# An opening in 176-token pieces with half weight blocks, and an ending in which the last two output blocks run by token half

## The chip, the cores and the metric

The kernel runs on all 8 cores of one Trainium2 chip, as two dies of four cores (cores 0 to 3 and 4 to 7). Each core computes half of one batch row, 2 × 1024 tokens, and the cores exchange nothing. The metric is the device time of the slowest core in microseconds (us).

Executions of this program fall into two states. In the slow state one die or both show a lower granted TensorE clock (as the profile records it, 1.00 being full speed), where the undisturbed runs have 0.996 to 0.999.

## The reference

One layer of a decoder trunk, in float32, with 16384 tokens of 2048 channels. The kernel works in bf16 on TensorE. What matters here is the first thing that is done and the last:

```python
def rmsnorm(x, g):
    y = x * lax.rsqrt(jnp.mean(x * x, axis=-1, keepdims=True) + EPS)
    return y * g

def swiglu_ffn(h, w_in, w_out):            # w_in: (2048, 2*5632), w_out: (5632, 2048)
    gate, up = jnp.split(h @ w_in, 2, axis=-1)
    return (jax.nn.silu(gate) * up) @ w_out

def reference(x, ...):                     # one layer
    x = x + 0.5 * swiglu_ffn(rmsnorm(x, ffn1_norm), ffn1_w_in, ffn1_w_out)
    x = x + mixer_block(rmsnorm(x, mix_norm), ...)      # [cut]
    x = x + 0.5 * swiglu_ffn(rmsnorm(x, ffn2_norm), ffn2_w_in, ffn2_w_out)
    return rmsnorm(x, final_norm)
```

The kernel must begin with the product of the norm of x with `ffn1_w_in`, and can end only after the last column of the last product has gone into the sum of squares of the final norm.

## The kernel before

Tokens lie along the free dimension and channels on the 128 partitions, so a token's sum of squares is a sum over 16 rows of channels and then over the partitions. The 16 rows are added by VectorE (or row by row on the way), and the partitions by a float32 matmul with a matrix of ones ("the sum" below). The norm factor is applied after the product, in the eviction from PSUM, so the product can begin with the raw x, only cast to bf16.

The opening takes x in three pieces of 352 tokens. Each weight block of 256 columns (1 MB in bf16) is one DMA.

```python
def x0_raw(s):                      # cast piece s into H (bf16): 12 rows on VectorE, 4 on ScalarE
    ...
def x0_sum(s, us):                  # squares on ScalarE, then adds of 4, 4, 4, 2, 1 rows on VectorE
    ...
    later(us, lambda: (pending.discard((0, s)), stats_finish(0, lo, hi)))   # the sum, root, reciprocal

x0_load(0)
first = [W.get(w1, 0, NKD, 0)]                       # one block of 256 columns
x0_load(1)
first += [W.get(w1, 0, NKD, DFF), W.get(w1, 0, NKD, 256), W.get(w1, 0, NKD, DFF + 256)]
x0_load(2)
x0_raw(0); x0_sum(0, 2.0); x0_raw(1)
# [cut] tiles in the order (block, piece), gate and up halves of two hidden blocks:
order = [(0, 0), (0, 1), (1, 0), (1, 1), (2, 0), (2, 1), (3, 0), (3, 1)]
order += [(w, 2) for w in range(4)]                  # piece 2 of all four blocks at the end
```

The ending is the last product, `ffn2_w_out` on the second 1024 tokens, in 8 blocks of 256 output columns. Blocks 0 to 6 run whole. Block 7 runs in three pieces of tokens, and the output of a piece is finished while TensorE works on the next one:

```python
cuts = (0, T // 2, T // 2 + 320, T)                  # pieces of 512, 320 and 192 tokens
# done(j, qs, bank): eviction with residual, square on ScalarE, add into RS on VectorE
# finish(q): the sum by ones, root, reciprocal;  final(q, sets): multiply 16 rows by RS, store
for q, (lo, hi) in enumerate(pieces):                # the last block
    for m in range(2):
        bank = nbank(True)
        for (k0, nk), ws in zip(kbs, wss):
            part(bank, ws, m, lo, hi, k0, nk)
            if q > 0 and m == 0 and k0 == 16:
                finish(q - 1)
                final(q - 1, sets[0:2])
        done(2 * cb + m, [q], bank)
        if q > 0 and m == 0:
            final(q - 1, sets[2:])                   # stands ahead of the eviction of m == 1
finish(npc - 1)
final(npc - 1, sets)
```

The program emits one list of instructions for each engine, with semaphores between the lists. In the traces below VectorE works off its list in the order of emission: on core 5 of after, casts whose data is there stand behind an eviction that waits 2.92 us.

Of the kernel before, what the change touches and what calls it, by code (L numbers as in the profile page):

```python
# [12 lines left out]
D = 2048  # L13
# [12 lines left out]
CUT = sorted({0, W0} | {c for g in GA + GB for c in g})  # L26
# [134 lines left out]
class WStream:  # L161
    def __init__(self, P, ring):
        self.P = P
        self.ring = ring
        self.n = 0
        self.bufs = [Buf(f"ring{i}") for i in range(RING)]
        self.semk = [P.newsem(f"ring{i}") for i in range(RING)]

    def get(self, wt, k0, nk, c0, reads=()):
        s = self.n % RING  # L170
        self.n += 1
        src = wt[c0 // 256, :, k0:k0 + nk, :]
        dst = self.ring[s]
        self.P.op(POOL, lambda e, dst=dst, src=src, nk=nk: e.dma_start(out=dst[:, 0:nk, :], in_=src),  # L174
                  reads=reads, writes=[self.bufs[s]], semkey=self.semk[s], incval=16)
        return s

    def pair(self, wt, cb, nk):
        s = self.n % RING
        self.n += 1  # L180
        src = wt[cb:cb + 2].rearrange("c p k n -> p c k n")
        dst = self.ring[s][:, 0:2 * nk, :].rearrange("p (c k) n -> p c k n", c=2)
        self.P.op(POOL, lambda e, dst=dst, src=src: e.dma_start(out=dst, in_=src),
                  writes=[self.bufs[s]], semkey=self.semk[s], incval=16)
        return s
# [14 lines left out]
def emit_program(nc, st, dr):  # L200
# [17 lines left out]
    ring = [sb(f"ring{i}", [128, 16, 256], BF16) for i in range(RING)]  # L218
# [24 lines left out]
    N0 = W0 // 3  # L243
    X0 = view(0, 48 * N0 * 4, F32, N0)
    b_X0 = [[region(f"X0{k}_{s}", (s * NKD + k) * 4 * N0, 4 * N0) for s in range(3)] for k in range(NKD)]
# [55 lines left out]
    s_x0 = [P.newsem(f"x0{s}{q}") for s in range(3) for q in range(4)]  # L301
# [3 lines left out]
    b_DW = {n: [Buf(f"d{n}_{c}") for c in range(8)] for n in ("WBc", "WBo")}  # L305
# [92 lines left out]
    def wcol(s, kc, m):  # L398
        return ring[s][:, kc, m * 128:(m + 1) * 128]

    def proj_H(ws, m, g):
        lo, hi = g
        bank = nbank()
        mms(bank, [(wcol(ws, k, m), H[:, k, lo:hi]) for k in range(NKD)],
            [W.bufs[ws]] + [b for k in range(NKD) for b in r_H[k].at(lo, hi)], True, True, hi - lo)
        return bank
# [62 lines left out]
    def to_bf16(src, dst, c):  # L469
        P.op(POOL, lambda e: e.dma_start(out=dr[dst][c], in_=dr[src][c]), writes=[b_DW[dst][c]], semkey=s_w,  # L470
             incval=16)
# [27 lines left out]
    def ffn_in(w_in, S, groups, first=None, hook=None, un=False, mid=None, conv=False, cast=()):  # L499
        tmps = {}  # L500

        def gate(ws, m, s):
            g = groups[s]
            n = g[1] - g[0]
            bank = proj_H(ws, m, g)

            def fn():
                t = mul_rs(bank, S, g) if un else None
                tmps[m, s] = t2 = t if un else ntmp()
                act(bank, tmp(t2, n), [b_TMP[t2]], AF.Silu, n, t=t)  # L510

            evac((S, s), bank, fn)
            run_bg()

        def up(ws, b, m, s):
            lo, hi = g = groups[s]
            n = hi - lo
            bank = proj_H(ws, m, g)
            j = 2 * b + m

            def fn():
                t = tmps[m, s]
# [12 lines left out]

        cast = deque(cast)
        if hook is None:
            first = [W.get(w_in, 0, NKD, 0), W.get(w_in, 0, NKD, DFF)]
            order = [(w, s) for s in range(len(groups)) for w in range(2)]
        else:  # L540
            order = [(0, 0), (0, 1), (1, 0), (1, 1), (2, 0), (2, 1), (3, 0), (3, 1)]
            order += [(w, 2) for w in range(4)]
        for i, (w, s) in enumerate(order):
            if hook is not None:
                hook(i)
            for m in range(2):
                if w % 2 == 0:
                    gate(first[w], m, s)
                else:
                    up(first[w], w // 2, m, s)  # L550
        for b in range(len(first) // 2, NKF // 2):
# [24 lines left out]
    def ffn_out(w_out, S, groups, src, dst, un_cg=None, hd=None, ahead=None):  # L576
        for cb in range(NKD // 2):
# [6 lines left out]
            for k0 in range(0, NKF, 16):  # L584
# [5 lines left out]
                for m in range(2):  # L590
                    j = 2 * cb + m
                    for s, (lo, hi) in enumerate(groups):
# [3 lines left out]
                            [W.bufs[ws]] + [b for k in range(nk) for b in r_A[k0 + k].at(lo, hi)],  # L596
# [15 lines left out]
    def ffn_out_last(w_out, S, src):  # L612
# [4 lines left out]
        nblk = 3 * NKD // 2  # L617
        spare = (W.n + nblk) % RING
        tw = TMP[:, NTMP - 2:NTMP, :].rearrange("p c t -> p (c t)")
        rows = [(ap[:, HALO:W0], bufs) for ap, bufs in rows]  # L620
        rows.append((ring[spare][:].rearrange("p k c -> p (k c)").bitcast(F32)[:, 0:T], [W.bufs[spare]]))
        rows.append((tw, b_TMP[NTMP - 2:NTMP]))
        state["tmp"] = 0
        cuts = (0, T // 2, T // 2 + 320, T)
# [14 lines left out]
        def done(j, qs, bank):  # L639
# [13 lines left out]
            else:  # L653
                t = turn("tmp", NTMP - 2)
# [19 lines left out]
        for j, n in ((0, 4), (4, 4), (8, 4), (12, 2), (14, 1), (15, 1)):  # L674
# [4 lines left out]
            elif j < 14:  # L679
                ap = sg[:, :, HALO:W0]  # L680
            else:
                ap = rows[j][0].unsqueeze(1)
# [17 lines left out]
        def part(bank, ws, m, lo, hi, k0, nk):  # L700
            lo, hi = lo + HALO, hi + HALO
            mms(bank, [(wcol(ws, k, m), ACTB[:, k0 + k, lo:hi]) for k in range(nk)],
                [W.bufs[ws]] + [b for k in range(nk) for b in r_A[k0 + k].at(lo, hi)],
                k0 == 0, k0 + nk == NKF, hi - lo)

        for cb in range(NKD // 2):
            last = cb == NKD // 2 - 1
            if last:
                wss = [W.get(w_out, k0, nk, cb * 256) for k0, nk in kbs]
            load(2 * cb)  # L710
            load(2 * cb + 1)
            if not last:
                halves = [(0, T // 2, [0]), (T // 2, T, list(range(1, npc)))]
                bk = [[nbank(True) for h in halves] for m in range(2)]
                for k0, nk in kbs:
                    ws = W.get(w_out, k0, nk, cb * 256)
                    for m in range(2):
                        for s, (lo, hi, qs) in enumerate(halves):
                            part(bk[m][s], ws, m, lo, hi, k0, nk)
                            if k0 + nk == NKF:  # L720
                                done(2 * cb + m, qs, bk[m][s])
                continue
            for q, (lo, hi) in enumerate(pieces):
                for m in range(2):
                    bank = nbank(True)
                    for (k0, nk), ws in zip(kbs, wss):
                        part(bank, ws, m, lo, hi, k0, nk)
                        if q > 0 and m == 0 and k0 == 16:
                            finish(q - 1)
                            final(q - 1, sets[0:2])  # L730
                    done(2 * cb + m, [q], bank)
                    if q > 0 and m == 0:
                        final(q - 1, sets[2:])
# [48 lines left out]
    def mix_a(S, hd):  # L782
# [125 lines left out]
        def grp(gi, ws):  # L908
            for m in range(2):
                j = 2 * gi + m  # L910
                for lo, hi in GB:
                    bank = nbank()
                    mms(bank, [(wcol(ws, 2 * gi + k, m), PLD[:, k, lo - HALO:hi - HALO]) for k in range(2)],
                        [W.bufs[ws]] + b_P, True, True, hi - lo)
# [15 lines left out]
        def pool_out(ws, j, g, i, gate, b_gate, k0=0):  # L930
            lo, hi = g
            bank = nbank()
            mms(bank, [(wcol(ws, k0 + k, j % 2), MX[:, k, lo:hi]) for k in range(8)],
                [W.bufs[ws]] + [b for k in range(8) for b in r_MX[k].at(lo, hi)], True, True, hi - lo)
# [25 lines left out]
        for j in range(12, NKD):  # L960
            i = turn("st", NST)
            for s, g in enumerate(GB):
                c = 2 * (j - 12) + s
                pool_out(wp, j, g, i, SG[:, c, :], b_SG[c], 8 * (j // 2 - 6))
# [76 lines left out]
    def mix_b(S, hd=None, un_cg=None):  # L1041
# [12 lines left out]
        for cb in range(8):  # L1054
            ws = W.get(dr["WBc"], 0, 8, cb * 256, [b_DW["WBc"][cb]])
            for m in range(2):
# [3 lines left out]
                for lo, hi in GB:  # L1060
# [4 lines left out]
                        [W.bufs[ws]] + [b for k in range(8) for b in cn(k)[1]], True, True, n)  # L1065
# [9 lines left out]
        for cb in range(8):  # L1075
# [3 lines left out]
            for m in range(2):  # L1079
# [3 lines left out]
                for k0, k1 in cuts:  # L1083
                    for s, (lo, hi) in enumerate(GB):
                        n = hi - lo
                        mms(bks[s], [(wcol(ws, k, m), MG[:, k, lo:hi]) for k in range(k0, k1)],
                            [W.bufs[ws]] + [b for k in range(k0, k1) for b in r_M[k].at(lo, hi)],
# [12 lines left out]
    def x0_load(s):  # L1100
        for q in range(4):
            P.op(POOL, lambda e, q=q: e.dma_start(  # L1102
                out=X0[:, s * NKD + 4 * q:s * NKD + 4 * q + 4, :], in_=dr["x0"][s, :, 4 * q:4 * q + 4, :]),
                writes=[b_X0[k][s] for k in range(4 * q, 4 * q + 4)], semkey=s_x0[4 * s + q], incval=16)

    def quad(s, q):
        k0 = s * NKD + 4 * q
        return X0[:, k0:k0 + 4, :], [b_X0[k][s] for k in range(4 * q, 4 * q + 4)]

    def x0_raw(s):  # L1110
        lo, hi = GA[s]
        for q in range(4):
            for k in range(4 * q, 4 * q + 4):
                src, b = X0[:, s * NKD + k, :], [b_X0[k][s], b_CST]
                if k % 4 == 3:
                    P.op(ACT, lambda e, k=k, src=src: e.activation(out=H[:, k, lo:hi], in_=src, func=AF.Copy,
                                                                   scale=cst(C_N1 + k)),
                         reads=b, writes=r_H[k].at(lo, hi))
                else:
                    vec(N0 / 2, lambda e, k=k, src=src: e.tensor_scalar(  # L1120
                        out=H[:, k, lo:hi], in0=src, scalar1=cst(C_N1 + k), scalar2=None, op0=ALU.mult),
                        b, r_H[k].at(lo, hi))

    def x0_sum(s, us):
        lo, hi = GA[s]

        def tree(n, out, in1, reads, writes):
# [175 lines left out]
```

## Time and profile before

| | |
|---|---|
| time, 3 fast runs | 5003.28, 5004.66, 5004.85 us (median 5004.66); a fourth run was slow, 5183.32 |
| profiled execution, slowest core 2 | span 5005.4 us (device time of this execution 5007.22) |
| spans of the 8 cores | 4997.5 to 5005.4 us, granted clock 0.996 to 0.998 |
| TensorE (PE) busy | 4933.7 us, 99% |

The head of the profile's page and the first group of its busy table:

```profile
span 5005.4 us, 63154 instructions; the slowest of 8 cores (4997.5 to 5005.4 us)
PE 4933.7 (99%) x24878; PEld 2477.3 (49%) x25230; DVE 1987.2 (40%) x2548; ACT 722.8 (14%) x1161; POOL 217.3 (4%) x414
```

TensorE is busy for 99% of the span, so only its idle time can be won without taking work away. The waits of TensorE, summed over the whole run of core 2, are few. The columns are the waiting line and tile, what it waited for, the total in us, how often, and the longest.

```profile
PE bank L392 <- DMA ring<-ffn_w_in: 21.9, 1, 21.9
PE bank L667 <- DVE RS L657: 12.6, 2, 7.7
PE bank L438 <- DVE RS L1128: 3.3, 1, 3.3
PE bank L392 <- DVE H L1120: 2.9, 1, 2.9
```

All of these lie at the two ends. The timeline of TensorE at the opening of core 2 follows. Its columns are start, duration, engine, line, operation, output and inputs, form, count, and in brackets the idle time before it with what ended it.

```profile
21.94 4.85 PE L392 MATMUL bank<-H,ring 128*128 128x352 bf16 x16 [21.94 <-DMA ring<-ffn_w_in]
...
33.12 11.39 PE L392 MATMUL bank<-H,ring 128*128 128x352 bf16 x64 [2.91 <-DVE H L1120]
47.83 1.32 PE L438 MATMUL bank<-RS,ONES 128*128 128x352 f32 x2 [3.31 <-DVE RS L1128]
48.94 11.24 PE L392 MATMUL bank<-H,ring 128*128 128x352 bf16 x66
```

The first matmul starts at 21.94 us, when its weight block has landed. After two more waits, for the casts into H and for the sum of squares (RS), TensorE is dense from 48.94 us on.

The same view at the ending, core 2:

```profile
4963.82 10.41 PE L392 MATMUL bank<-BIG,ring 128*128 128x320 bf16 x88
4981.96 1.40 PE L667 MATMUL bank<-RS,ONES 128*128 128x320 f32 x2 [7.73 <-DVE RS L657]
4983.16 6.71 PE L392 MATMUL bank<-BIG,ring 128*128 128x192 bf16 x56
4994.76 0.98 PE L667 MATMUL bank<-RS,ONES 128*128 128x192 f32 x2 [4.89 <-DVE RS L657]
```

The sums wait 7.73 and 4.89 us for RS. The timeline of VectorE (DVE) in the first of these waits tells why:

```profile
4969.66 4.49 DVE L692 TENSOR_TENSOR H<-H,RS 128x2048 f32<-128x2048 f32 x2
...
4975.64 2.28 DVE L692 TENSOR_TENSOR XS<-XS,RS 128x2048 f32<-128x2048 f32 x1
...
4979.57 0.68 DVE L692 TENSOR_TENSOR TMP<-TMP,RS 128x512 f32<-128x512 f32 x1
4980.18 0.48 DVE L647 SCALAR_TENSOR_TENSOR TMP<-bank,TMP 128x320 f32<-128x320 f32 x1
4981.32 0.49 DVE L657 TENSOR_TENSOR RS<-RS,TMP 128x320 f32<-128x320 f32 x1 [0.67 <-ACT TMP L655]
```

The bank with the last row of the 320-token piece is complete at about 4974.2 us (4963.82 + 10.41). Its eviction, the write into TMP at 4980.18, stands behind output multiplies of the 512-token piece (L692), for which TensorE is not waiting. The sum can start only after the add at 4981.32.

### The profile page before, as it was taken

What the parts mean: (1) busy time and instruction counts of PE and PEld (TensorE: products, weight loads), DVE (VectorE), ACT (ScalarE), POOL (GpSimd) and SP (SyncE); (2) the same over time, 40 slices, a digit from 0 to 9 for tenths busy, and PEclk for the clock granted to TensorE, in tenths of its full rate; (3) what the DMA queues carried; (4) which work ended last, traced back from release to release, by engine and by line L of the source; (5) the groups of instructions that cost most, each with busy time, mean ns of one, the idle gap of its engine ahead of it and who ended that gap; (6) DMA issues with size and microseconds to landing.
All of it is one profiled execution on the core that took longest, in us unless ns stands there. A gap on an engine that the chain in (4) does not pass through costs nothing.

```text
span 5005.4 us, 63154 instructions; the slowest of 8 cores (4997.5 to 5005.4 us)
## 1 busy us (share of the span) xinstructions
PE 4933.7 (99%) x24878; PEld 2477.3 (49%) x25230; DVE 1987.2 (40%) x2548; ACT 722.8 (14%) x1161; POOL 217.3 (4%) x414
## 2 busy tenths in 40 slices
PE   7999999999999999999999999999999999999998
PEld 4666666665444444444444444444444444444444
DVE  5344421289980000322568994001141533333113
ACT  3111111112110000121112210000020120000111
POOL 0000000000000000000000000000000000000000
PEclk9999999999999999999999999999999999999999
DMA  7768856545574444566766675344565754555544
GB/s 156 131 127 149 149 103 130 126 74 114 110 143 91 80 72 82 126 158 168 239 144 140 141 151 101 68 82 71 117 147 131 237 128 86 120 109 113 132 75 114
DMA packets 147795, 617.24 MB, mean 123 GB/s; under 512 B 14384, under 2 KB 37040, under 8 KB 107184
## 3 DMA queue, kind: packets, MB, share of 16 engines
q0 software_dynamic: 57632, 394.55, 45.5%
q1 hardware_dynamic: 89872, 218.64, 12.3%
q8 instruction: 204, 3.34, 0.3%
q14 instruction: 87, 0.71, 0.1%
HBM read 877.37 MB, written 109.05 MB: 197 GB/s over the span
## 4 chain that ended last, share of the span: by engine, by line
PE 98%; issue 1%; DVE 1%; DMA 1%; ACT 0%; POOL 0%; DVEq 0%; ACTq 0%; POOLq 0%
PE bank L392 97%; DMA BIG<-x 1%; PE bank L438 0%; DVE RS L671 0%; DVE BIG L1128 0%; DVE RS L448 0%; DVE H L692 0%; POOL BIG L1102 0%; PE bank L667 0%; ACT L446 0%; ACT BIG L1134 0%; DVE ST L692 0%; ACT TMP L655 0%; ACT RS L669 0%; DVE TMP L476 0%
## 5 line engine op out<-in xcount | busy, mean ns | idle before, releaser
L392 PE MATMUL bank<-H,ring 128*128 128x512 bf16 (+1 forms) x16852 | 3344.6, 358 | 40.0 <-DMA ring<-ffn_w_in 21.9
L392 PEld LDWEIGHTS bank<-H,ring 128*128 128x128 bf16 x17088 | 1673.6, 98 | 1692.0 <-issue 32.8
L392 PE MATMUL bank<-BIG,ring 128*128 128x512 bf16 (+2 forms) x7910 | 1584.1, 360 | 6.1
L392 PEld LDWEIGHTS bank<-BIG,ring 128*128 128x128 bf16 x8024 | 786.8, 98 | 795.2 <-issue 19.6
L792 DVE SCALAR_TENSOR_TENSOR BIG<-BIG,CST 128x1024 f32<-128x1024 f32 x480 | 595.5, 1277 | 0.0
L529 DVE TENSOR_TENSOR BIG<-bank,TMP 128x512 bf16<-128x512 f32 x176 | 121.8, 692 | 990.0 <-PE bank L392 989.9
L476 DVE TENSOR_TENSOR TMP<-bank,RS 128x512 f32<-128x512 f32 (+1 forms) x468 | 288.4, 617 | 405.5 <-PE bank L392 403.9
L600 DVE SCALAR_TENSOR_TENSOR XS<-bank,XS 128x512 f32<-128x512 f32 (+1 forms) x112 | 69.0, 616 | 538.8 <-PE bank L392 538.8
L524 DVE TENSOR_TENSOR TMP<-bank,TMP 128x352 f32<-128x352 f32 (+1 forms) x220 | 130.0, 591 | 382.6 <-PE bank L392 379.5
L489 ACT ACTIVATE TMP<-TMP 128x352 f32<-128x352 f32 (+1 forms) x220 | 120.3, 549 | 1027.6 <-DVE TMP L476 1027.5
L489 ACT ACTIVATE TMP<-bank 128x512 f32<-128x512 f32 x176 | 105.1, 597 | 1089.6 <-PE bank L392 1089.6
L433 DVE TENSOR_TENSOR RS<-RS,TMP 128x512 f32<-128x512 f32 (+1 forms) x223 | 143.2, 657 | 226.9 <-ACT TMP L431 226.9
L174 POOL DMA_DIRECT2D ring<-ffn_w_in x176 | 93.5, 532 | 2304.1 <-PE bank L392 2280.3
L526 DVE TENSOR_TENSOR BIG<-TMP,RS 128x352 bf16<-128x352 f32 (+1 forms) x220 | 130.4, 593 | 24.1 <-DVE TMP L524 2.4
L431 ACT ACTIVATE TMP<-XS 128x512 f32<-128x512 f32 (+1 forms) x147 | 83.2, 576 | 220.2 <-DVE XS L600 203.5
L489 ACT ACTIVATE TMP<-TMP,CST 128x512 f32<-128x512 f32 (+1 forms) x88 | 60.2, 685 | 344.7 <-DVE TMP L476 344.7
L174 POOL DMA_DIRECT2D ring<-ffn_w_out x96 | 50.7, 528 | 1216.1 <-PE bank L392 1191.2
L573 ACT ACTIVATE H<-XS,CST 128x352 bf16<-128x352 f32 (+1 forms) x56 | 34.0, 607 | 348.0 <-DVE XS L600 278.1
L448 DVE RECIPROCAL RS<-RS 128x512 f32<-128x512 f32 (+1 forms) x20 | 59.9, 3030 | 30.5 <-ACT RS L446 30.3
L489 ACT ACTIVATE ST<-TMP,CST 128x512 bf16<-128x512 f32 x64 | 46.2, 722 | 170.4 <-DVE TMP L476 164.9
L174 POOL DMA_DIRECT2D ring<-w_in x56 | 29.6, 528 | 791.6 <-PE bank L392 791.6
L647 DVE SCALAR_TENSOR_TENSOR H<-bank,H 128x512 f32<-128x512 f32 x16 | 11.1, 692 | 120.3 <-PE bank L392 120.3
(90 smaller groups left out, 893.9 us busy)
## 6 DMA issues: line engine op xcount, KB each, us to landing
ring<-ffn_w_in POOLq DMA_DIRECT2D x176, 1024.0 KB, 9.9
ring<-ffn_w_out POOLq DMA_DIRECT2D x64, 1024.0 KB, 10.1
ring<-w_in POOLq DMA_DIRECT2D x56, 1024.0 KB, 10.5
XS<-X SPq DMA_DIRECT2D x60, 512.0 KB, 12.2
X<-XS SPq DMA_DIRECT2D x56, 512.0 KB, 6.0
XS<-x SPq DMA_DIRECT2D x48, 512.0 KB, 10.4
ring<-ffn_w_out POOLq DMA_DIRECT2D x32, 768.0 KB, 7.6
ring<-WBo POOLq DMA_DIRECT2D x16, 1024.0 KB, 8.2
```

Of the source, the lines that this page charges most:

```text
L174: self.P.op(POOL, lambda e, dst=dst, src=src, nk=nk: e.dma_start(out=dst[:, 0:nk, :], in_=src), reads=reads, writes=[self.bufs[s]], semkey ...
L392: ins = e.matmul(d, w, r, start=(start and i == 0), stop=(stop and i == last))
L431: P.op(ACT, lambda e: e.activation(out=tmp(t, hi - lo), in_=src, func=AF.Square), reads=sbufs, writes=[b_TMP[t]])
L433: vec(hi - lo, lambda e: e.tensor_tensor(out=rs, in0=rs, in1=tmp(t, hi - lo), op=ALU.add), b_rs + [b_TMP[t]], b_rs)
L448: vec((hi - lo) * 6, lambda e: e.reciprocal(out=rs, in_=rs), b_rs, b_rs)
L476: vec(hi - lo, lambda e: e.tensor_tensor(out=tmp(t, hi - lo), in0=banks[bank][:, 0:hi - lo], in1=rsg(S, lo, hi), op=ALU.mult), [b_bank[ban ...
L489: P.op(ACT, lambda e: e.activation(out=out, in_=src, func=func, **kw), reads=[sbuf, b_CST], writes=obufs)
L524: vec(n, lambda e: e.tensor_tensor(out=tmp(t, n), in0=banks[bank][:, 0:n], in1=tmp(t, n), op=ALU.mult), [b_bank[bank], b_TMP[t]], [b_TMP[t]])
L526: vec(n, lambda e: e.tensor_tensor(out=ACTB[:, j, lo:hi], in0=tmp(t, n), in1=rsg(S, lo, hi), op=ALU.mult), [b_TMP[t]] + r_RS[S].at(lo, hi) ...
L529: vec(n, lambda e: e.tensor_tensor(out=ACTB[:, j, lo:hi], in0=banks[bank][:, 0:n], in1=tmp(t, n), op=ALU.mult), [b_bank[bank], b_TMP[t]], ...
L600: vec(n, lambda e, x=x, bank=bank, n=n: e.scalar_tensor_tensor(out=x, in0=banks[bank][:, 0:n], scalar=0.5, in1=x, op0=ALU.mult, op1=ALU.ad ...
L792: vec(T, lambda e: e.scalar_tensor_tensor(out=C[:, c, :], in0=G[:, j, 2 + t:2 + t + T], scalar=cst(C_CVK + j * KCONV + t), in1=C[:, c, :], ...
```

## The change

The intent is to start the first product sooner, with smaller first loads, and to keep TensorE from waiting for VectorE at the end. The cuts below are marked; the rest of the diff adapts names, buffers and the layout of the weights (blocks of 128 columns).

```diff
--- before, the opening
+++ after
-    N0 = W0 // 3                       # x in three pieces of 352 tokens
+    N0 = W0 // 6                       # six pieces of 176
...
+    def half(self, s, m, wt, c0):      # half a weight block, 128 columns, 512 KB in bf16
+        self.load(s, self.ring[s][:, m], wt[c0 // 128 + m], [self.bufs[s][m]], (self.semk, self.semh)[m][s])
...
-    x0_load(0)
-    first = [W.get(w1, 0, NKD, 0)]
-    x0_load(1)
-    first += [W.get(w1, 0, NKD, DFF), W.get(w1, 0, NKD, 256), W.get(w1, 0, NKD, DFF + 256)]
-    x0_load(2)
+    for what in ("x0", (0, 0), "x1", (1, 0), (0, 1), "x2", (1, 1), "x3", (2, 0), (3, 0), "x4", (2, 1), (3, 1), "x5"):
...
...                                     # cut: before, adds of 4, 4, 4, 2, 1 rows for 352 tokens
+            n = 8                       # per piece of 176 tokens: adds of 8, 4, 2, 1 rows
+            while n:
+                ...
+                n //= 2
...
+        tile(0, 0, 0)                   # tile(piece, block, half): 16 matmuls of 176 tokens
+        tile(1, 0, 0)
+        both(0, 1, 0)                   # both(p, ...): pieces 2p and 2p+1
+        both(0, 0, 1)
+        x0_raw(2)
+        x0_stats(0)
+        tile(2, 0, 0)
+        tile(2, 1, 0)
+        tile(2, 0, 1)
+        both(0, 1, 1)
+        tile(2, 1, 1)
+        x0_raw(3)
+        x0_sum(1)
+        tile(3, 0, 0)
+        ...
--- before, the ending
+++ after
-        cuts = (0, T // 2, T // 2 + 320, T)
+        cuts = (0, T // 2, T // 2 + 256, T // 2 + 416, T)
...
+        block(6, whole[0:1], w_late)    # first 512 tokens of blocks 6 and 7
+        block(7, whole[0:1], w_late)
+        bk = [nbank(True) for m in range(2)]
+        for k0, nk in kbs:              # second 512 tokens of block 6
+            ws = w_late(6, k0, nk)
+            for m in range(2):
+                part(bk[m], ws, m, T // 2, T, k0, nk)
+            if k0 == 0:
+                finish(0)
+                final(0, sets[0:2])     # the large multiply hides behind these matmuls
+            elif k0 == 16:
+                final(0, sets[2:])
+        for m in range(2):
+            done(12 + m, whole[1][2], bk[m])
+        wss = [w_late(7, k0, nk) for k0, nk in kbs]
+        for q in range(1, npc):         # second 512 tokens of block 7: 256, 160, 96
+            ...
--- before, ffn_in of the second ffn
+++ after
-    ffn_in(dr["ffn2_w_in"], 1, GB, un=True, mid=lambda: final_stream(0, 25.0))
+    ffn_in(dr["ffn2_w_in"], 1, GB, un=True, mid=lambda: final_stream(0, 25.0),
+           cast=[("ffn2_w_out", "WBf", c) for c in range(4)])    # last weights cast to bf16 in DRAM early
```

The work on TensorE stays the same in columns; the opening has twice as many matmuls, each half as wide, and the weights of blocks 6 and 7 are read twice.

## The prediction

> **Bound:** TensorE, busy 4933.7 of 5005.4 us (busy table); between 93.7 and 4902 us it is busy 4787 of 4808 us (windows). Only the two ends can win.
>
> *Opening* (timeline): the first matmul starts at 21.94, as the 1 MB weight block lands behind 2.9 MB of x. Before 49 us PE then waits 2.9 us for the VectorE casts into H and 3.3 us for the sum of squares; some runs cold (first 16 matmuls of 352 took 4.85 us, the next 16 2.55). From 48.94 it is dense; the first two weight pairs end at about 93.7.
>
> *Ending*: PE waits 7.73 and 4.89 us for the RS sums (PE waits), because VectorE runs the output multiplies (2.28 us each at 512 tokens) ahead of the evictions; the clock is then 0.64-0.67 (windows). The last product matmul ends at 4989.9, the span at 5005.4.
>
> **Opening after.** Source data arrived at about 0.34 MB/us (17 MB by 56 us). First tile needs 1.44 MB x and 1.05 MB weights: estimate 13.4 us instead of 21.9. But then VectorE paces. My estimate for a 176-token cast is 0.24 us (352: 0.34), so 2.9 us a piece, and 7.8 us for the adds of two pieces (1408-wide add 1.62, 704 0.89, 352 0.53). Walk: casts of piece 1 end 19; sums 0 and 1 end 29; casts of piece 2 end 32; reciprocal 2.35 and evictions; casts of piece 3 end about 44, with 36 of 48 tiles left at 1.21 us each (estimate 75.8 ns a matmul, from 148.8 at 352). Two sums and a wait for evictions (2-3 us) follow: end about 91 (88.5 to 94). Most of the 8.5 us is lost waiting for VectorE. Gain 2.7 us (0 to 7).
>
> [...]
>
> **Ending after.** Blocks 6 and 7 take the first half first, so the whole multiply of 512 tokens (about 13 us VectorE) hides behind block 6's second half (19 us). From the end of block 5 at 4901.8: three times 19.0, one sum 0.8, pieces 9.6 + 6.1 + 3.7 [...] plus two sums. VectorE walk for the tail: PE waits about 1 us before sum 2 and about 4.5 before the last sum; reciprocal of 96 about 0.75 (192: 1.35, 320: 2.15), one multiply and one output DMA fewer: end about 4994.5. Gain 11 us (7 to 13). The last weights (0.75 MB, 7.5 us landing) load while outputs move at about 340 GB/s; it may stall PE up to 3 us.
>
> **Middle.** Twice the weight descriptors, and four casts of 2.9 MB in the weight queue: nothing, landing is 10 us against over 19 us of slack.
>
> **Predicted: 4991 us, 80%: 4983 to 4998.** Faster by over 2%: 0.01; within 2%: 0.97; slower by over 2%: 0.02.
>
> **Shows it:** first matmul near 13.5; in PE waits, H casts and RS sums of opening total over 8 us; opening tiles end near 91; PE waits at the RS sums of the ending under 7 us in total; time from last product matmul to span end 12-13 us; matmul of 176 near 76 ns warm.
>
> **Wrong if:** narrow matmuls are bound by weight loads; 384-byte output rows slow the last stores; VectorE order stalls the opening more than walked.

The sum: 5005.4 − 2.7 − 11 is 4991.7. The 75.8 ns for a matmul of 176 tokens is an estimate; a line through two widths in the traces of before gives the same (1960 matmuls of 352 in 292.53 us on core 2, 149.2 ns each; 832 of 512 in 179.74 us on core 0, 216.0 ns).

## The result, and the profile after

The fast runs beside those of before took 4992.14 and 4993.49 us, and a further fast one 4993.38. Executions in which one die ran at a lower clock are left out of the means. The ratio of the fast runs is 0.9978, with a 95% interval of 0.9955 to 1.0: same at the 2% threshold. Ratios here are the mean time of one kernel's fast runs over that of the other's fast runs of the same rounds, so not quite the ratio of the medians that are quoted.

The slowest core of the profiled execution is core 5 (cores 4986.4 to 4990.6 us, granted clock 0.997 to 0.999):

```profile
span 4990.6 us, 64591 instructions; the slowest of 8 cores (4986.4 to 4990.6 us)
PE 4949.1 (99%) x25704; PEld 2503.6 (50%) x25704; DVE 1993.5 (40%) x2600; ACT 726.1 (15%) x1178; POOL 294.0 (6%) x428
```

Busy time of TensorE *rose* by 15.4 us while the span fell by 14.8. More matmul records are in this trace (25704, as many as weight loads; before has 24878 for 25230 weight loads), and a busy TensorE is not always at one rate (on core 5, 16 matmuls of 176 took 157 ns each from 14.14 us on and 128 took 77 each from 85.00), so the busy sum cannot tell what was gained. For that I split every execution at two places that are at the same position in the work in all kernels: "M1", the start of the first pair of 512-token sums after the opening's product (about 372 us), and the start of the last eviction of output row 11, the end of block 5 (about 4897 us). The three lengths, as means over the 8 cores of the profiled execution:

| | start to M1 | M1 to end of block 5 | end of block 5 to the end | sum |
|---|---|---|---|---|
| before | 372.07 | 4525.78 | 103.48 | 5001.34 |
| after | 372.68 | 4523.50 | 92.74 | 4988.93 |
| difference | +0.6 | −2.3 | −10.7 | −12.4 |

So the ending brought nearly everything, and the opening nothing. The −2.3 us in the middle does not look like the change's work: in this one execution of before, cores 0 to 3 took 4526.5 to 4529.0 us for the middle and cores 4 to 7 only 4523.8 to 4524.2, which is 1.8 us on the mean of all eight. The windows view of core 2 shows a granted clock of 0.92 from 2100 to 2170 us, where core 5 shows 1.00, with TensorE busy for 69.6 and 70.0 of the 70 us; core 2 of the kernel after shows 1.00 there. In windows of 10 us, cores 0 to 3 all show 0.81 from 2110 to 2120, and cores 2 and 3 once more from 2150 to 2160.

The waits of TensorE after, core 5:

```profile
PE bank L1186 <- DMA ring<-ffn_w_in: 14.1, 1, 14.1
PE bank L1186 <- DVE H L1143: 8.4, 3, 3.4
PE bank L675 <- DVE RS L665: 5.9, 2, 4.0
PE bank L1186 <- DVE TMP L487: 2.8, 1, 2.8
...
PE bank L445 <- DVE RS L1163: 1.1, 1, 1.1
```

The wait for the first weights fell from 21.9 to 14.1 us, and that for RS at the ending (L667, now L675) from 12.6 to 5.9. The opening's wait for its sums (L438, now L445) fell from 3.3 to 1.1. But its waits for casts into H went up from 2.9 to 8.4 us, and a wait for evictions (TMP) of 2.8 us is new there.

*Opening.* The timeline of TensorE, core 5; line 1186 holds the opening's tiles:

```profile
14.14 2.51 PE L1186 MATMUL bank<-H,ring 128*128 128x176 bf16 x16 [14.14 <-DMA ring<-ffn_w_in]
20.08 8.10 PE L1186 MATMUL bank<-H,ring 128*128 128x176 bf16 x80 [3.43 <-DVE H L1143]
...
32.01 10.15 PE L1186 MATMUL bank<-H,ring 128*128 128x176 bf16 x96 [1.93 <-DVE H L1143]
45.19 8.73 PE L1186 MATMUL bank<-H,ring 128*128 128x176 bf16 x96 [3.03 <-DVE H L1143]
...
59.76 24.78 PE L1186 MATMUL bank<-H,ring 128*128 128x176 bf16 x320 [2.79 <-DVE TMP L487]
...
85.00 9.87 PE L1186 MATMUL bank<-H,ring 128*128 128x176 bf16 x128
94.71 2.55 PE L399 MATMUL bank<-H,ring 128*128 128x352 bf16 x16
```

The first matmul starts 7.8 us earlier than on core 2 of before, and the product is dense only from 59.76 us instead of 48.94. The opening's tiles end at 94.71 us, on the mean of the cores at 93.44. Before they ended at about 92.9 on the mean (M1 less 279.2 us, the distance between the two places in the kernels that ran here).

What VectorE does before the longest of these waits, the one that ends at 45.19:

```profile
41.12 0.53 DVE L531 TENSOR_TENSOR TMP<-bank,TMP 128x352 f32<-128x352 f32 x1 [2.92 <-PE bank L1186]
41.75 0.53 DVE L533 TENSOR_TENSOR BIG<-TMP,RS 128x352 bf16<-128x352 f32 x1
42.19 2.74 DVE L1143 TENSOR_SCALAR H<-BIG,CST 128x176 bf16<-128x176 f32 x12
```

The casts of piece 3 (the 12 `TENSOR_SCALAR` at 42.19) stand behind the eviction at 41.12, and that has waited 2.92 us for a bank that TensorE was still filling. When TensorE has filled it, it has nothing left but tiles of piece 3, and now it waits for VectorE to evict and to cast. The two engines take turns. How long a turn lasts differs, and the clock has a part in it: on core 5 the granted clock read 0.50 from 32 to 36 us, and the 96 matmuls from 32.01 on took 10.15 us. On cores 0 and 2, at 1.00, they took 7.44 us; there VectorE idled 1.97 and 0.69 us in the same evictions, and both waits are put down to ScalarE (L500, a table load of 1.28 us and an activation of 0.50) and not to TensorE. So ScalarE is a link of the chain as well. On five of the eight cores, 1, 3, 4, 5 and 7, it is TensorE that the second of these evictions waits for (1.86 to 2.92 us). The order of VectorE's list shows here too: ScalarE's share of the casts of piece 3 ran at 38.70 us on this core without a wait for data, but VectorE's share only at 42.19, with 2.92 us of idle time on the way.

*Ending.* TensorE of core 5 and below it the output multiply of the 512-token piece on VectorE:

```profile
4943.48 24.90 PE L399 MATMUL bank<-BIG,ring 128*128 128x512 bf16 x188
...
4968.69 5.08 PE L399 MATMUL bank<-BIG,ring 128*128 128x160 bf16 x88
4975.68 0.51 PE L675 MATMUL bank<-RS,ONES 128*128 128x160 f32 x2 [1.91 <-DVE RS L665]
4976.03 3.08 PE L399 MATMUL bank<-BIG,ring 128*128 128x96 bf16 x44
4983.13 0.71 PE L675 MATMUL bank<-RS,ONES 128*128 128x96 f32 x2 [4.02 <-DVE RS L665]
```

```profile
4949.32 4.49 DVE L700 TENSOR_TENSOR H<-H,RS 128x2048 f32<-128x2048 f32 x2
...
4957.07 1.22 DVE L700 TENSOR_TENSOR TMP<-TMP,RS 128x1024 f32<-128x1024 f32 x1
4958.20 0.68 DVE L655 SCALAR_TENSOR_TENSOR ST<-bank,ST 128x512 f32<-128x512 f32 x1
```

The multiplies from 4949.32 to 4958.3 us run beside 24.9 us of matmuls that need nothing from VectorE (the line merges matmuls of 512 tokens with those of the 256-token piece). The sums of the last two pieces wait 1.91 and 4.02 us instead of 7.73 and 4.89; over the cores of after these waits total 5.4 to 7.0 us. On core 2 of before the last product matmul ended 88.0 us after the end of block 5 (4983.16 + 6.71 − 4901.91), and the span 15.5 us after that; on core 5 of after it is 81.1 us (4976.03 + 3.08 − 4898.00) and 11.5. So 6.9 us came from what runs before the last product matmul, mostly the first wait (5.8 us less), and 4.1 from the tail, where the last piece is 96 instead of 192 tokens wide.

### The profile page after: what moved, and what is told of

It is laid out like the page before. It is cut to its first block, busy times and chain, and to the rows that moved or that the text cites. A ratio compares the mean times of both kernels' runs of the same rounds, so it can differ in the third digit from the quotient of the medians.

```text
span 4990.6 us, 64591 instructions; the slowest of 8 cores (4986.4 to 4990.6 us)
## 1 busy us (share of the span) xinstructions
PE 4949.1 (99%) x25704; PEld 2503.6 (50%) x25704; DVE 1993.5 (40%) x2600; ACT 726.1 (15%) x1178; POOL 294.0 (6%) x428
## 4 chain that ended last, share of the span: by engine, by line
PE 98%; DVE 1%; issue 0%; DMA 0%; ACT 0%; POOL 0%; DVEq 0%; ACTq 0%; POOLq 0%
PE bank L399 97%; PE bank L1186 1%; PE bank L445 0%; DMA BIG<-x 0%; DVE BIG L1163 0%; DVE H L1143 0%; DVE RS L455 0%; ACT L453 0%; DVE RS L679 0%; DVE XS L610 0%; DVE H L700 0%; ACT TMP L438 0%; DVE XS L700 0%; ACT BIG L1154 0%; POOL BIG L1130 0%
## 5 line engine op out<-in xcount | busy, mean ns | idle before, releaser
L399 PE MATMUL bank<-H,ring 128*128 128x512 bf16 (+1 forms) x16704 | 3294.1, 359 | 2.3 <-DVE TMP L487 1.3
L399 PEld LDWEIGHTS bank<-H,ring 128*128 128x128 bf16 x16704 | 1634.4, 98 | 1642.4 <-issue 5.8
L399 PE MATMUL bank<-BIG,ring 128*128 128x512 bf16 (+3 forms) x8112 | 1586.0, 357 | 0.0
L500 ACT ACTIVATE TMP<-TMP 128x352 f32<-128x352 f32 (+1 forms) x220 | 120.5, 549 | 1024.3 <-DVE TMP L487 1024.2
L500 ACT ACTIVATE TMP<-bank 128x512 f32<-128x512 f32 x176 | 105.1, 597 | 1089.6 <-PE bank L399 1089.6
L176 POOL DMA_DIRECT2D ring<-ffn_w_in x180 | 125.6, 700 | 2269.2 <-PE bank L399 2173.0
L176 POOL DMA_DIRECT2D ring<-ffn_w_out x90 | 63.2, 702 | 1122.9 <-PE bank L399 1093.6
L438 ACT ACTIVATE TMP<-XS 128x512 f32<-128x512 f32 (+1 forms) x147 | 83.2, 576 | 220.5 <-DVE XS L610 203.8
L500 ACT ACTIVATE TMP<-TMP,CST 128x512 f32<-128x512 f32 (+1 forms) x88 | 60.3, 686 | 344.7 <-DVE TMP L487 344.7
L1186 PE MATMUL bank<-H,ring 128*128 128x176 bf16 x768 | 66.6, 254 | 25.4 <-DMA ring<-ffn_w_in 14.1
L1186 PEld LDWEIGHTS bank<-H,ring 128*128 128x128 bf16 x768 | 65.0, 104 | 27.5 <-issue 27.2
```

What stands on the lines that cost most here:

```text
L176: self.P.op(POOL, lambda e: e.dma_start(out=dst, in_=src), reads=reads, writes=bufs, semkey=sem, incval=16)
L399: ins = e.matmul(d, w, r, start=(start and i == 0), stop=(stop and i == last))
L438: P.op(ACT, lambda e: e.activation(out=tmp(t, hi - lo), in_=src, func=AF.Square), reads=sbufs, writes=[b_TMP[t]])
L500: P.op(ACT, lambda e: e.activation(out=out, in_=src, func=func, **kw), reads=[sbuf, b_CST], writes=obufs)
L1186: ins = e.matmul(d, wcol(first[w], k, m), H[:, k, lo:hi], start=k == 0, stop=k == NKD - 1)
```

## The experiments

Theory A: the gain is the ending's; the opening gains nothing because VectorE paces it, in a chain of turns between VectorE and TensorE (casts behind evictions, evictions behind tiles, the sum behind the adds). Rival B: the narrow matmuls and half blocks cost what the early start wins, so that VectorE is not the limit. Rival C, a part of A: the amount of VectorE's work, that is the adds of the sum of squares, is the limit, and not its order. For the ending, the rivals are the order (token halves), the smaller last pieces and the early cast.

The experiments ran in three batches, each on a chip of its own beside runs of before: e_end to e_order, then e_order2 to e_oldseq, then e_nocast, e_best and e_again. The six profiled executions with the change's opening (after, e_open, e_pieces, e_oldseq, e_nocast, e_again) have M1 at 372.68 to 374.05 us, mean 373.40; the two with the old opening (before, e_end) at 372.07 and 371.83. That spread of 1.4 us is what a difference in M1 has to exceed. It also puts the new opening at 1.4 us slower than the old rather than the 0.6 of the first pair.

### The ending alone, and the opening alone

e_end is the kernel after with the opening of before; e_open is the kernel after with the ending of before and without the early cast. The edit of each puts back the corresponding functions:

```diff
# e_end, against after
-    N0 = W0 // 6
+    N0 = W0 // 3
...  # x0_load, x0_sum, the list of tiles and the first weight loads as in before
# e_open, against after
...  # ffn_out_last as in before, no cast of ffn2_w_out
```

> The changed kernel with the old opening (pieces of 352 tokens, whole weight blocks, four x loads a piece), the new ending kept. My theory (the ending brings all of it, the opening nothing): 4992 us, within 2 us of the changed kernel; mean over the cores of the start of the first pair of 512-token sums about 372 us; from the last eviction of output row 11 to the end of the span 92.9 us. Rival (the opening brings a good part, some 3 to 5 us, hidden by other differences): 4995 to 4998 us.

> The changed kernel with the old ending (blocks whole, pieces 512, 320, 192, no early cast of the last weights), the new opening kept. My theory: 5003 to 5005 us, no faster than before; sums mark at about 372.7 us mean of the cores; row 11 to end 103.5 us. Rival: 4998 to 5001 us.

| | fast runs, us | to M1 | middle | end |
|---|---|---|---|---|
| before, same chip | 5001.8, 5001.9, 5002.59 (also 5025.32 and 5053.37) | | | |
| e_end | 4993.36, 4993.6 | 371.83 | 4524.66 | 92.86 |
| e_open | 5003.44, 5004.21, 5004.68 | 373.61 | 4523.43 | 103.87 |

Two runs of before, 5025.32 and 5053.37, were counted as fast but have a disturbed die (lowest mean clock 0.992 and 0.986). They spoil the ratios (e_end 0.9946, interval 0.9845 to 1.0046; e_open 0.9966, interval 0.9866 to 1.0067). Beside the three undisturbed runs, e_end is 8.6 us faster (mean 5002.1 to mean 4993.5), and e_open 2 us slower. The marks say the same: e_end has the ending of after (92.86 us) and e_open that of before (103.87). The ending is shown to carry the gain, and the opening to carry none, within the spread of M1.

### Less work in VectorE's adds

e_notree takes away most of the adds of the opening's sum of squares. It gives wrong numbers (relative error 0.67), and everything else stays.

```diff
-            n = 8
+            n = 1
```

> The changed kernel with three of the four adds of each sum-of-squares tree in the opening left out (wrong numbers on purpose), 6.5 us of VectorE per pair of pieces. Theory A (the order of VectorE's queue delays the casts of piece 3: they stand behind an eviction that waits for TensorE): the adds are mostly not what TensorE waits for, sums mark only 1 to 2 us earlier than 372.7. Theory B (VectorE's amount of work delays it): sums mark 5 us or more earlier.

This was one execution, and cores 4 to 7 were disturbed in it (5039.64 us). Cores 0 to 3 have M1 at 373.39 us, and the same cores of after at 372.79: no gain, where 1 to 2 us had been expected, though each piece has some 3 us less of adds (on core 0 of after the three large adds of a piece take 3.25 us). The timeline of TensorE on core 0:

```profile
42.58 9.95 PE L1186 MATMUL bank<-H,ring 128*128 128x176 bf16 x96 [3.92 <-DVE RS L1163]
```

And core 0 of after, for comparison:

```profile
43.69 9.09 PE L1186 MATMUL bank<-H,ring 128*128 128x176 bf16 x96 [3.51 <-DVE H L1143]
...
58.62 26.12 PE L1186 MATMUL bank<-H,ring 128*128 128x176 bf16 x320 [2.79 <-DVE TMP L487]
```

The wait before the tiles of piece 3 is still there, 3.92 us. (The releaser named is the last semaphore seen; on core 0 of after the same wait of 3.51 us is put down to the casts into H.) VectorE's timeline of core 0 tells what became of the time:

```profile
27.36 1.42 DVE L1143 TENSOR_SCALAR H<-BIG,CST 128x176 bf16<-128x176 f32 x6 [2.99 <-DMA BIG<-x]
29.55 1.41 DVE L1143 TENSOR_SCALAR H<-BIG,CST 128x176 bf16<-128x176 f32 x6 [0.78 <-DMA BIG<-x]
...
39.59 2.74 DVE L1143 TENSOR_SCALAR H<-BIG,CST 128x176 bf16<-128x176 f32 x12
```

Without the adds VectorE reaches the casts of piece 2 early, but their data lands only then: it idles 2.99 and 0.78 us for x. The casts of piece 3, at 39.59, come after the evictions as before, and the tiles of piece 3 start at 42.58 us instead of 43.69 on core 0 of after. Of these 1.1 us, 0.9 go at once, as the next 96 matmuls take 9.95 instead of 9.09 us, and the dense stretch starts at 58.38 instead of 58.62 us. Cutting the adds alone is thus worth 0.2 us on this core, and rival C falls as the whole story: right behind the adds stand the arrival of x, the order of the queue and the wait for a bank. What these 96 matmuls take differs from core to core by more than this 0.2 us (9.01 to 10.03 us on cores 0 to 3 of e_notree, 7.44 to 9.09 on those of after), so the small number itself is not sharp.

### The order of VectorE's queue

e_order moves the casts of piece 3 ahead of the evictions; no work is added or removed. e_order2 also spreads the tiles so that a bank is free when it is needed.

```diff
# e_order, against after
         tile(2, 0, 1)
+        x0_raw(3)
         both(0, 1, 1)
         tile(2, 1, 1)
-        x0_raw(3)
         x0_sum(1)
# e_order2, against e_order
         x0_stats(1)
+        both(0, 3, 0)
+        state["bank"] = 7
         both(1, 2, 0)
-        for w, m in ((3, 0), (2, 1)):
-            for p in range(2):
-                both(p, w, m)
+        state["bank"] = 4
+        both(1, 3, 0)
+        for p in range(2):
+            both(p, 2, 1)
```

> The changed kernel with the casts of piece 3 put into the queues ahead of the eviction of the fourth tile of the first 352 tokens; no work is added or taken away. Theory A: the 3.0 to 3.5 us wait of TensorE for the casts of piece 3 goes, sums mark about 3 us earlier (369.7), the 2.8 us wait for a bank eviction stays. Theory B: under 1 us.

> As e_order, and the tiles after the second sum are taken in an order that uses a PSUM bank that has long been free (one more tile of the first 352 tokens before it). Nothing is added or taken away. Chain theory (the waits of TensorE in the opening are links of one chain on VectorE and PSUM; a wait that is taken away is partly replaced by the next): the 2.8 us wait for a bank eviction goes and nothing takes its place, sums mark 3 us earlier than e_order, about 369; time 4988 to 4990 us. Rival (TensorE pays by cold clock and narrow matmuls, not by waits): sums mark stays at 372.

All three runs of e_order were slow, two through cores 4 to 7 and one (5746.75 us) through cores 0 to 3. In the profiled one cores 0 to 3 ended at 4987 to 4989 us, with M1 at 372.24 (after, same cores: 372.79). I had expected 369.7, and it missed. The timeline of its core 0 shows where the rest went:

```profile
41.84 7.44 PE L1186 MATMUL bank<-H,ring 128*128 128x176 bf16 x96 [1.66 <-DVE H L1143]
50.94 0.83 PE L445 MATMUL bank<-RS,ONES 128*128 128x352 f32 x2 [1.66 <-DVE RS L1163]
...
56.98 18.18 PE L1186 MATMUL bank<-H,ring 128*128 128x176 bf16 x233 [2.79 <-DVE TMP L487]
```

The wait for the casts is 1.66 us, where core 0 of after has 3.51, but the sum now waits 1.66 us for its adds, which it did not before, and the wait of 2.79 us for a bank stands unchanged. The wait was handed on. (M1 of this core is 3.0 us earlier than in after, but not through waits: here the 96 matmuls took 7.44 us instead of 9.09, and the 320 after the wait for a bank 24.78 instead of 26.12.)

e_order2, core 0:

```profile
33.59 17.45 PE L1186 MATMUL bank<-H,ring 128*128 128x176 bf16 x192 [1.93 <-DVE H L1143]
...
57.84 7.51 PE L1186 MATMUL bank<-H,ring 128*128 128x176 bf16 x96 [0.36 <-DVE TMP L487]
```

Here 192 matmuls run through without the wait for piece 3, and the 2.79 us for a bank have become 0.36. They take 17.45 us, where twice the 7.44 us of 96 matmuls at a granted clock of 1.00 is 14.9. That the clock was low here, as it was on core 5 of after where 96 took 10.15 us, is an estimate from these times. Later waits of 0.62, 0.46 and 1.28 us are new. M1 is 371.22 us, 2.2 us before the mean of the change's opening and outside its spread, but not the 369 that I had expected, as the new waits take part of the gain. Its undisturbed runs took 4990.22 and 4991.98 us (before on this chip 5002.0 to 5003.26); two more, 5012.94 and 5012.73, have disturbed cores.

### Both together

e_both is e_order2 with `n = 1`, again with wrong numbers.

> e_order2 with three of the four adds of each sum-of-squares tree left out as well (wrong numbers on purpose). Chain theory: the two waits for sums that e_order showed (about 1.3 and 1.7 us) go too, sums mark 366 to 367, so both cuts together bring more than each alone (0 and 0.5 us). Rival: 372.

It took 4987.61 us in its one execution, with M1 at 368.63 (366 to 367 had been expected). Taking the adds away alone moved M1 not at all, the order alone by −2.2, and both by −4.8 us against the mean of 373.40. Independent costs would add up, and these don't. But M1 mixes two things, and the traces keep them apart. The table splits the opening of the profiled executions, from the start to the end of its tiles, as means over the 8 cores (before: the end is M1 less 279.2):

| us | first matmul starts | later waits of TensorE | sums | matmuls | end of tiles |
|---|---|---|---|---|---|
| before | 22.2 | 6.4 | 2.4 | 61.9 | 92.8 |
| after | 14.6 | 11.9 | 2.1 | 64.9 | 93.4 |
| e_order2 | 14.9 | 10.2 | 2.1 | 64.7 | 92.0 |
| e_both | 14.8 | 9.5 | 2.0 | 63.1 | 89.4 |
| e_best (below) | 14.9 | 8.9 | 3.8 | 63.2 | 90.8 |

The six executions with the change's opening have 11.8 to 12.6 us of later waits and 64.9 to 65.5 of matmuls. In waits, the adds alone brought nothing (e_notree, cores 0 to 3: 12.0, and after the same), the order 1.6 us, and both 2.4. This is how a chain behaves in which the next wait takes over when one is cut, and it fits theory A. The other 1.8 us of e_both against after lie in the matmuls: on core 0 of e_both both runs of 96 took 7.44 us, what 96 take on core 0 of after at a granted clock of 1.00 (32.74 to 40.18 us). Whether the shorter waits are the reason was not tested: a wait of 1.93 us was followed by a granted clock of 0.50 on core 5 of after (32 to 36 us) and of 1.00 on core 0.

Rival B as a whole falls: with the same half blocks and 176-token matmuls the opening is 3.4 us earlier than the old one (M1 368.6 against 372.0) once VectorE's waits are shorter, and e_best below gets 2 us of that with right numbers. But a part of it is true. The matmuls of after take 2.9 us longer than those of before. Narrowness alone is some 1.0 us of this: from the first start to the start of what follows, 128 matmuls of 176 took 9.71 us on core 0 of after (75.9 ns each), and 128 of 352 on core 2 of before 19.09 us (half of one is 74.6), which over 768 matmuls makes 1.0. The rest, 1.9 us, fits more time in stretches such as the one from 32.01 us on core 5 (0.50, 10.15 us for 96 matmuls), but was not isolated.

### The ending: pieces, order, early cast

e_pieces keeps the order of the change with the old pieces of 320 and 192 tokens. e_oldseq is e_open (the old order) with the new pieces of 256, 160 and 96. e_nocast is after, with the last weights read as float32 and cast by the load as before.

```diff
# e_pieces, against after
-        cuts = (0, T // 2, T // 2 + 256, T // 2 + 416, T)
+        cuts = (0, T // 2, T // 2 + 320, T)
# e_oldseq, against e_open
-        cuts = (0, T // 2, T // 2 + 320, T)
+        cuts = (0, T // 2, T // 2 + 256, T // 2 + 416, T)
# e_nocast, against after
-            return W.get(dr["WBf"], k0, nk, (cb - 6) * 256, b_DW["WBf"][2 * cb - 12:2 * cb - 10])
+            return W.get(w_out, k0, nk, cb * 256)
...  # and no cast=[("ffn2_w_out", "WBf", c) ...]
```

> The changed kernel with the old pieces of 320 and 192 tokens in the new order of the ending. Order theory (the token-half order brings the ending's gain, because the 512-token multiply hides behind block 6; the number of pieces matters little since VectorE's work in the tail grows with each piece): from row 11 to end 92 to 94.5 us, time within 2 us of the changed kernel. Rival (the small last piece brings it): 97 us or more.

> e_open with the new pieces of 256, 160 and 96 tokens in the old order of the ending. Order theory: from row 11 to end 101 to 104 us, no gain from the pieces. Rival: 97 us or less.

> The changed kernel without the early cast of the last two output blocks' weights: they are loaded and cast from the float32 input each time, twice for the two token halves. The early cast made these loads land in 5.5 us instead of 10. If the cast is needed (my prediction feared a wait of up to 3 us for the last weights while the outputs move): TensorE waits for the ring in the ending, 1 to 4 us, from row 11 to end 94 to 97 us. If not: no wait for the ring, 92.5 to 93.5 us.

| ending | length from the end of block 5, us | fast runs, us |
|---|---|---|
| old order, old pieces (before; e_open) | 103.48; 103.87 | |
| old order, new pieces (e_oldseq) | 105.46 | 5005.28 |
| new order, old pieces (e_pieces) | 93.64 | 4993.93, 4993.95, 4995.75 |
| new order, new pieces (after; e_end) | 92.74; 92.86 | |
| new order, new pieces, no early cast (e_nocast) | 94.17 (93.1 to 96.9) | 4998.46 |
| the same with the early cast, same chip (e_again) | 93.10 | 4995.22, 4995.96, 4996.06 |

The new order, with the early cast, brings about 9.8 us (103.5 to 93.6), the smaller pieces 0.9 more in the new order, and in the old order they lose 2 us (expected were 101 to 104 us for e_oldseq): each piece adds a sum, and to VectorE's queue a reciprocal and the multiplies of its 16 rows, and there they stand ahead of evictions. On core 2 of e_oldseq the three sums wait 9.27, 3.22 and 3.99 us, where two wait 7.73 and 4.89 on core 2 of before. The ratio of e_pieces to before is 0.9984 (0.9965 to 1.0004).

Without the early cast, core 6 has this wait in its list, which e_again does not have:

```profile
PE bank L399 <- DMA ring<-ffn_w_out: 2.7, 1, 2.7
```

Cores 0 and 3 have such a wait too in this one execution, of 1.5 and 1.2 us. Core 6 lost 3.3 us in the ending (96.87 against 93.58), the mean of the cores 1.1. The last loads of 768 KB took 8.4 to 8.8 us to land from float32 (cores 0, 3 and 6) and 4.6 to 4.9 from the bf16 copy (the eight cores of after; medians by core).

### A version that beats both

e_best adds three things to e_order2, and its numbers are right. VectorE makes only the first, 8-row add of each piece and writes it in bf16; TensorE adds the 8 rows and the partitions in 16 matmuls of 176 with ones in bf16 (1.38 us where the float32 pair takes 0.83). ScalarE casts 6 of 16 rows instead of 4. The casts of pieces 4 and 5 are spread between tiles.

```diff
-            n = 8
-            while n:                                    # adds of 8, 4, 2, 1 rows
-                ...
+            vec(8 * N0, lambda e, s=s, x=x, y=y: e.tensor_tensor(
+                out=SQ[:, 8 * s:8 * s + 8, :], in0=x, in1=y, op=ALU.add), b + c, [b_SQ[s]])
...
+            for h in range(2):
+                for k in range(8):
+                    ins = e.matmul(banks[bank][:, h * N0:(h + 1) * N0], ONEB[:], SQ[:, 8 * (2 * p + h) + k, :],
+                                   start=k == 0, stop=k == 7)
...
-            if k % 4 == 3:                              # rows cast by ScalarE
+            if k % 8 in (2, 5, 7):
```

> e_order2 with less VectorE work in the opening and a right result: VectorE does only the first add of each tree, into bf16, and TensorE sums the other eight rows with a bf16 matrix of 1/2048 (16 matmuls of 176, about 1.25 us, in place of one float32 sum of 0.8); ScalarE casts 6 of 16 rows of a piece in place of 4; the casts of pieces 4 and 5 stand between tiles. VectorE loses about 3.9 us of adds per pair of pieces and 0.5 us of casts per piece. Chain theory: sums mark near 369 (e_both, with wrong numbers, 368.6; e_order2 371.2), time 4988 to 4990 us. Rival: 371 or later, 4991 us or more.

> The changed kernel itself, on the same chip as e_best and e_nocast, for comparison. Fast runs at 4992 to 4995 us; sums mark 372.7 to 374 us, from row 11 to end 92.7 us.

The result is correct. The fast runs of e_best took 4992.35, 4992.61, 4994.15 and 4994.68 us, those of e_again (the kernel after, again) 4995.22, 4995.96 and 4996.06, and before on this chip 5005.49 and 5006.25. From the means (4993.45, 4995.75, 5005.87) e_best is 2.3 us faster than the change and 12.4 us faster than before, a ratio of 0.9975. The expected 4988 to 4990 us, with M1 near 369, were missed: M1 is at 370.00 us against 373.54 in e_again; the middle, which the edit does not touch, was 0.5 us longer in this execution.

## Why the prediction was right or wrong

**The total.** 4991 us were predicted, and the fast runs show 4992.1 to 4993.5, inside the range; the class is the predicted one. That it came so close is luck, as errors partly cancel: the opening gave nothing where 2.7 us were expected; the profiled execution of before, from whose 5005.4 us I subtracted, had lost some 1.8 us on the mean of its cores, and more on its slowest, in a stretch of lower clock that the next execution didn't have; and 5005.4 is a span, 1.8 us less than the device time of the same execution.

**The bound: right.** Only the ends could win, and the middle did not move by the change.

**The ending: right.** Predicted gain 11 us (7 to 13), measured 10.7. The waits for RS are 5.9 us on core 5 and 5.4 to 7.0 over the cores (under 7 predicted), though the split on core 5 was 1.9 and 4.0 rather than 1 and 4.5. From the last product matmul to the end of the span there are 11.5 us, a little less than the 12 to 13 predicted. That the late weights could stall TensorE by up to 3 us was a warning about the kernel as it is, which after does not show; it is what e_nocast shows once the early cast is taken out (2.7 us on core 6). So the early cast is worth its while, by the one execution without it.

**The opening's start: right in kind, slightly off.** First matmul predicted at 13.4 us; measured 14.1 to 15.1 by core, mean 14.63 (before: 22.16).

**The opening's mechanism: right in the main, and incomplete.** "VectorE paces" and "most of the 8.5 us is lost waiting for VectorE" are what the trace and e_both show: of the 7.5 us that the product starts earlier, 5.5 go into longer waits. But 2.9 go into slower matmuls (the sums take 0.3 less), for which the walk had no term beyond their width. Casts of piece 3 were predicted to end at about 44 us and ended at 44.9; waits for casts and sum were predicted over 8 us and were 9.5 (8.4 + 1.1). A matmul of 176 tokens was predicted near 76 ns and took 75.9 at a granted clock of 1.00 (core 0 of after, 128 from 85.21 us; 77.1 if the time is counted to the recorded end of the last).

**The opening's size: wrong.** The failed step is "Two sums and a wait for evictions (2-3 us) follow: end about 91 ... Gain 2.7 us". On core 5 the tiles ended at 94.71. The terms that were too small, from 44 us on: the start of piece 3's tiles 1.2 us later (45.19); the first 96 matmuls after that wait took 8.73 us where 96 take 7.44 at a granted clock of 1.00 (1.3 us); the further 480 cost 1.3 ns more each than estimated (0.6 us); and the two sums (0.6 us each net) with the 2.79 us for a bank come to 4.0 us where the walk left 3.4 (0.6 us). Together 3.7 us. The walk treated each wait as a pause after which matmuls run at once at full rate. The trace of core 5 shows that they do not: the 16 matmuls at 14.14 took 2.51 us, 157 ns each, and after the wait before 45.19 the granted clock read 0.50 for almost 2 us. The prediction names such a stretch for before ("cold": 4.85 us for the first 16 matmuls of 352, 2.55 for the next) and counted none for after. Besides, I took 93.7 us of the slowest core as the old end, where the mean core ends at about 92.9.

**What I had not seen.** The casts of piece 3 stand behind an eviction that waits for TensorE. I walked VectorE's work as if its own durations set the pace, and found about the right time by luck, as for part of it VectorE was idle (on core 5 for 1.97 us, waiting for ScalarE, and for 2.92 us, waiting for TensorE). This fits that cutting its work alone gained nothing (e_notree) and that the work and the order had to be changed together (e_both).

**What stays open.** The waits that remain in e_order2 and e_best were not cut one by one, so I can't say which is the next limit. What makes the granted clock read 0.50 after one wait and 1.00 after another of the same length (1.93 us on cores 5 and 0 of after) was not tested either. About 1 us of the ending's 6.9 us before the last product matmul was not traced to a cause.

## What to carry to other kernels

Look at what stands *behind* an instruction that waits for another engine: here its position in the queue cost more than the amount of work there (M1 2.2 us earlier by the order alone in e_order2, no gain from some 3 us less of adds a piece in e_notree), and a large multiply that TensorE does not wait for belonged beside matmuls that need nothing from its engine (the new order of the ending: 9.8 us). Earlier data and smaller pieces gained nothing where another engine paced the stretch (first matmul 7.5 us earlier, end of the opening's tiles 0.6 later), and they cost something in every matmul (75.9 ns at 176 tokens against 74.6 for half of one at 352), in waits after which the clock read 0.50 (10.15 us for 96 matmuls instead of 7.44), and, in the old order of the ending, in every sum (e_oldseq, 2 us). Where the waits form a chain, cutting one hands it to the next, so try the cuts together before giving up on each. Finally, when a change touches two per mille of the time and executions differ by as much, compare marks at the same position in the work instead of totals.

## Further measurements

- Width of a matmul: on core 0 of after, 128 matmuls of 176 took 9.87 us (77.1 ns each), 44 of 96 took 2.03 us (46 ns) and 1120 of 512 took 241.90 us (216 ns; from 2116.17 us), all at a granted clock of 1.00, counted to the recorded end of the last. The trace of the slowest core has a weight load for each matmul (25704 of both). Down to 96 tokens a narrower matmul took less time, so the fear of narrow matmuls that are bound by their weight loads did not come true.
- The granted clock and the rate: the first 16 matmuls of 176 took 157 ns each against 77.1 later, but the granted clock of this profile reads 1.00 in that very stretch (windows view, core 0 of after, 15.07 to 17.58 us), while it reads 0.50 in later slow stretches (core 5, 32 to 36 us, and 45.19 to 47). So the slow stretch at the very start had to be read from the mean duration of its matmuls.
- Dense work on all cores: in the profiled executions of before and after, with eight cores at it and the slowest of them 99% busy, the mean granted clock was 0.996 to 0.999. A clock of 0.81 does occur in stretches: in this execution of before on cores 0 to 3 from 2110 to 2120 us, and on cores 2 and 3 from 2150 to 2160, when cores 0 and 1 read 1.00. What starts such a stretch was not tested.
- Rows of the last stores: those of after have rows of 384 bytes (96 tokens in float32) and landed in 2.0 to 2.5 us, where the 768-byte rows of before took 2.2 to 3.3. No penalty is visible at these sizes, 96 to 192 KB a store against 96 to 384; at 96 KB it is 2.0 and 2.3 against 2.2 and 3.1. Both include the time behind other stores.
